# Gated ConvFFN of a two-layer trunk: the order of the seven products and of ScalarE's and VectorE's work in the up-projections

## The chip, the cores and the metric

The kernel runs on one core of one Trainium2 chip. The metric is the device time of one execution in microseconds, the median of several runs. TensorE is called PE, VectorE DVE, ScalarE ACT, GpSimd POOL, and SyncE, whose queue issues nearly all transfers, SP.

## The reference

A trunk of two layers works on 1024 tokens of width 1024, in float32. Layer 0 mixes tokens by a gated linear recurrence, layer 1 by attention over a window. Each layer ends with the part that the change is about, a gated ConvFFN of inner width 2816, followed by a layer norm:

```python
def conv_ffn(h, w_in, conv_w, conv_b, w_out):
    u = h @ w_in
    C = u.shape[-1]
    u = lax.conv_general_dilated(u, conv_w[:, None, :], window_strides=(1,),
                                 padding=[(CONV_WIDTH - 1, 0)],
                                 dimension_numbers=('NWC', 'WIO', 'NWC'),
                                 feature_group_count=C) + conv_b
    a, b = jnp.split(u, 2, axis=-1)
    return (jax.nn.silu(a) * b) @ w_out
```

So `u` (1024 tokens x 5632 channels) is made by a matrix product, each channel is convolved causally with three taps, the first half of the channels goes through SiLU and gates the second half, and a second matrix product goes back to width 1024.

## The kernel before

All products of matrices are made of three matmuls (`mm3`, lines 172 to 177): each operand is held as a high part and a low part in a rounded float32 format, and high x high, high x low and low x high are added in PSUM. The high part is a cast by ACT, the low part a subtraction by DVE (`split`, `low_part`: lines 201 and 148).

The up-projection (class `Up`) handles 22 chunks of 128 channels of each half, so a chunk `fc` gives a 2 x 2 block matrix C: C11 and C21 (the `a` half, for the first and the last 512 tokens; row 0 of a pair of rows of the tile `Y`) and C12 and C22 (the `b` half; row 1). The pair is `Y[:, 0:2]` for even chunks and `Y[:, 2:4]` for odd ones. C is not made of eight block products but of seven, in Strassen's manner (Winograd's form): sums and differences of blocks of the tokens are made once, in `TX` and `TZ`; differences of blocks of the weights are made for each chunk (`weight_sums`, DVE lines 412 to 415, each followed by casts and low parts into `HL` or `HT`). A product is four `mm3`, 12 matmuls of 512 columns. The products are numbered 1 to 7.

From chunk 2 on, the products share PSUM banks (`chained`, line 451). A bank A takes product 1, and then 6, 7 and 4 are added to it in place; after each of them the running sum is copied out by ACT, into C11 (line 457), C12 (463 is the copy into C22 and 461 the one into C12), C22 and C21 (466). PE may not add the next product before the copy has been made. A bank B takes product 2, which DVE adds to C11; a bank M takes product 5, which DVE adds to C22, then product 3 is added to M and DVE adds M to C12. The order in a chunk is 2, 6, 5, 7, then product 1 of the next chunk, 4, 3. Chunks 0 and 1 go another way (`run`, `collect`): each product has a bank of its own, ACT copies product 1 into both C11 and C12, and DVE does all the rest of the additions; product 3 of both chunks comes ahead of product 1 of chunk 2.

When C11 and C21 are there (after product 4), and when C12 and C22 are there (after product 3), `convolve` runs: one tap and the bias by ACT (line 499), two taps by DVE (501), and then SiLU by ACT (504) for the first half, or the product with the gate by DVE (506) and a store to `gd` in HBM for the second. The second half's convolution writes into `C[:, 0]`, the row of C11 and C21 of its own chunk, as scratch.

Beside this, each chunk makes a part of the differences of `ffn_w_out` that the down-projection will need (`down_sums`): load into `Y[:, 6]`, four subtractions of 256 columns by DVE (432), store to `bsd`. `Y[:, 7]` and three tiles `raw` take the loads of the weights (line 403).

PE issues in the order of the source; on ACT, DVE and SP a scheduler decides the order when the kernel is built, guided by priorities (`urgent()`). An engine works through its queue strictly in that order, so an instruction that waits holds up all behind it.

Of the kernel before, what the change touches and what calls it, by code (L numbers as in the profile page):

```python
# [16 lines left out]
P = 128  # L17
# [6 lines left out]
FF = 2816  # L24
# [61 lines left out]
def trunk(ctx: ExitStack, tc: tile.TileContext, a: dict, out: bass.AP):  # L86
# [246 lines left out]
    class Up:  # L333
        def __init__(self, l, pool, rx):
            self.l, self.rx = l, rx
            self.wv = a["ffn_w_in"][l].rearrange("(kc p) c -> p kc c", p=P)
            first = pool.tile([P, 2, 2, 4, 512], F32R, name="TX")
            self.pair = first
            self.TX = [first[:, 0], first[:, 1], pool.tile([P, 2, 4, 512], F32R, name="TZ")]
            self.W, self.raw, self.pieces, self.turned = {}, {}, 0, set()  # L340

# [45 lines left out]
        def weight_load(self, fc):  # L387
# [3 lines left out]
            ws = [whole((0 if fc % 2 else 8) + i) for i in range(7)]  # L391
            self.W[fc] = ws
# [11 lines left out]
            split(blocks(0, 0), blocks(0, 1), r1)  # L404
            self.raw[fc] = blocks, r1, r2

        def weight_sums(self, fc):
            blocks, r1, r2 = self.raw.pop(fc)
            b11, b21, b12, b22 = r1[:, 0], r1[:, 1], r2[:, 0], r2[:, 1]
            ws = self.W[fc]  # L410
            split(ws[6][:, :512], ws[6][:, 512:], b22)
# [4 lines left out]
            split(blocks(1, 0), blocks(1, 1), r1)  # L416
            last = lambda: split(blocks(2, 0), blocks(2, 1), r2)
            if fc:
                last()
            else:  # L420
                self.last = last

        def down_sums(self, n):
            (i, q), pairs = divmod(n, 2), FF // 256
            quarter = lambda rows: rows.rearrange("p (b q n) -> p b q n", b=2, q=2)[:, :, q, :]
            own = Y[:, 6, :].rearrange("p (k b n) -> p k b n", k=2, b=2)
            for k in range(2):
                row = (k * pairs + i) * P
                nc.sync.dma_start(own[:, k], quarter(a["ffn_w_out"][self.l][row:row + P, :]))
            (b11, b12), (b21, b22) = [(own[:, k, 0], own[:, k, 1]) for k in range(2)]  # L430
            for x, y, z in ((b11, b12, b11), (b12, b22, b12), (b22, b22, b11), (b21, b21, b22)):
                tt(x, y, z, op=sub)  # L432
            for k in range(2):
                nc.sync.dma_start(quarter(bsd[self.l][:, i, k, :]), own[:, k])
# [16 lines left out]
        def chained(self, p, fc, banks):  # L451
            A, B, M = banks
# [3 lines left out]
            if p == 1:  # L456
                nc.scalar.copy(C11, A)
            elif p == 2:
                tt(C11, C11, B, op=add)
            elif p == 6:  # L460
                nc.scalar.copy(C12, A)
            elif p == 7:
                nc.scalar.copy(C22, A)  # L463
                tt(C22, C22, M, op=add)
            elif p == 4:
                nc.scalar.copy(C21, A)
            elif p == 3:
                tt(C12, C12, M, op=add)
            if p in (4, 3):
                self.convolve(p, fc, C)  # L470

        def collect(self, p, fc, ps):
            C = Y[:, 2 * (fc % 2):2 * (fc % 2) + 2, :]
            C11, C21, C12, C22 = C[:, 0, :512], C[:, 0, 512:], C[:, 1, :512], C[:, 1, 512:]
            if p == 1:
                nc.scalar.copy(C11, ps)
                nc.scalar.copy(C12, ps)
            elif p == 2:
                tt(C11, C11, ps, op=add)
            elif p == 6:  # L480
                tt(C12, C12, ps, op=add)
            elif p == 7:
                tt(C22, C12, ps, op=add)
            elif p == 4:
                tt(C21, C22, ps, op=add)  # L485
            elif p == 5:
                both = C[:, 1, :].rearrange("p (h n) -> p h n", h=2)
                tt(both, both, ps.unsqueeze(1).to_broadcast([P, 2, 512]), op=add)
            elif p == 3:
                tt(C12, C12, ps, op=add)  # L490
            if p in (4, 3):
                self.convolve(p, fc, C)

        def convolve(self, p, fc, C):
# [3 lines left out]
            c = C[:, 0, :] if part else ca  # L498
            nc.scalar.activation(c, u, AF.Identity, bias=cwt[:, l, 3, ci:ci + 1], scale=cwt[:, l, 2, ci:ci + 1])  # L499
            for sh in (1, 2):  # L500
                nc.vector.scalar_tensor_tensor(c[:, sh:], u[:, :S - sh], cwt[:, l, 2 - sh, ci:ci + 1],  # L501
                                               c[:, sh:], op0=ALU.mult, op1=ALU.add)
            if part == 0:
# [5 lines left out]
        def run(self, ready, down):  # L509
# [5 lines left out]
            for (p, fc), ps in zip([(p, fc) for p in (4, 5) for fc in range(2)], ax):  # L515
                self.product(p, fc, ps)
# [8 lines left out]
            for (p, fc), ps in zip([(p, fc) for p in (1, 2) for fc in range(2)], mm):  # L525
                self.collect(p, fc, self.product(p, fc, ps))
            for fc in range(2):
                self.collect(6, fc, self.product(6, fc, mm[fc]))
            for fc in range(2):
                self.collect(7, fc, self.product(7, fc, mm[2 + fc]))  # L530
                self.collect(4, fc, ax[fc])
                self.collect(5, fc, ax[2 + fc])
            self.weight_load(2)
            for fc in range(2):
                self.product(3, fc, mm[fc])
                if fc == 0:
                    with urgent():
                        self.weight_sums(2)
                self.collect(3, fc, mm[fc])
            banks, n = mm[2:] + ax[:2] + mm[:2] + ax[2:], 0  # L540
            held, made = {}, 0
            todo = [(1, 2)]
            for fc in range(2, NF):
                todo += [(p, fc) for p in (2, 6, 5, 7)] + [(1, fc + 1)] * (fc < NF - 1) + [(4, fc), (3, fc)]
            for p, fc in todo:
                if p == 1 and fc > 2:
                    self.weights(fc)
                if p in (1, 2, 5):
                    held.setdefault(fc, []).append(banks[n % 8])
                    n += 1  # L550
                self.chained(p, fc, (held[fc] + [None, None])[:3])
                if p == 7 or p == 2 and fc in (8, 15):
                    self.down_sums(made)
                    made += 1
                if fc == NF - 1 and p in (2, 5, 4):
# [897 lines left out]
```

## Time and profile before

| | |
|---|---|
| median of 3 runs | 2175.99 us (2174.64 to 2178.3) |
| the profiled execution | 2177.97 us, its span 2175.8 us |
| PE busy | 2133.9 us, 98% |
| DVE busy | 1604.3 us, 74% |
| ACT busy | 934.0 us, 43% |
| granted clock, mean | 0.993 |
| products of the up-projection of layer 0 | 565 to 1003 us of the span |

How to read the rows that follow: a row of the waits says which engine waited, at which line, for which engine and line, how long in total, how often, and the longest. A row of the timeline gives the start in us, the duration, the engine, the line, the operation, what it writes and reads, and in brackets the idle time before it with what ended it. A row of the groups gives the count, the busy time, the mean in ns, and the idle time before. In a row of busy time by stretch stand, after the length, the busy us of each engine with its count of instructions that touch the stretch, then the clock that TensorE was granted, the share of the DMA engines and their rate. A busy PE is not PE at its peak: matmuls overlap, and their rate is read from their starts.

### The profile page before, as it was taken

How to read it: one execution, taken by the hardware profiler on the slowest of the kernel's cores; microseconds unless marked ns; L12 is line 12 of the kernel's file. 1: busy time of each engine (PE TensorE's matmuls, PEld its weight loads, DVE VectorE, ACT ScalarE, POOL GpSimd, SP SyncE). 2: the span in 40 equal slices, each digit the busy share in tenths (PEclk: the TensorE clock that was granted, in tenths of full speed). 3: DMA queues.
4: the chain of work that ended last, by engine and by line, in shares of the span. 5: the costliest groups of instructions: out<-in, count | busy, mean ns of one | idle time of the engine just before them, and what ended most of it. 6: DMA issues, size and time to landing. Idle time of an engine off the chain costs nothing.

```text
span 2175.8 us, 32521 instructions
## 1 busy us (share of the span) xinstructions
PE 2133.9 (98%) x12907; PEld 1788.7 (82%) x12907; DVE 1604.3 (74%) x2170; ACT 934.0 (43%) x1496; POOL 201.3 (9%) x194
## 2 busy tenths in 40 slices
PE   9999999999989999999999999999799999999998
PEld 8888888878868888888788888888688888888887
DVE  3655545468988888887987546769978888878986
ACT  3333333342445444445433246743534444454430
POOL 1221112120100000000001123312000000000002
PEclk9999999999999999999999999999999999999999
DMA  4111111132334444448854411242344444459662
GB/s 161 39 40 40 40 40 35 40 136 78 111 131 136 145 145 141 145 132 282 294 181 164 118 34 36 62 136 78 116 160 133 132 137 145 146 183 321 229 211 97
DMA packets 263698, 278.98 MB, mean 128 GB/s; under 512 B 31481, under 2 KB 201210, under 8 KB 263546
## 3 DMA queue, kind: packets, MB, share of 16 engines
q1 hardware_dynamic: 263032, 276.77, 38.7%
q8 instruction: 101, 1.65, 0.3%
q14 instruction: 51, 0.42, 0.1%
q10 hardware_dynamic: 450, 0.12, 0.0%
q0 software_dynamic: 64, 0.02, 0.0%
HBM read 213.91 MB, written 62.95 MB: 127 GB/s over the span
## 4 chain that ended last, share of the span: by engine, by line
PE 62%; DVE 7%; DMA 3%; issue 1%; ACT 1%; SPq 0%; DVEq 0%; ACTq 0%
PE psmm L174 11%; PE psmm L176 11%; PE psmm L175 11%; PE psax L174 8%; PE psax L175 8%; PE psax L176 8%; PE psmm L180 1%; DVE T L148 1%; PE psax L1232 1%; DVE Y L501 1%; PE psmm L184 1%; DMA raw<-in_ffn_w_out_dram 1%; DVE HL L148 1%; DMA gd<-Y 1%; DMA R<-bsd 1%
## 5 line engine op out<-in xcount | busy, mean ns | idle before, releaser
L174 PE MATMUL psmm<-T,HL 128*128 128x512 f32 x896 | 356.1, 397 | 2.8 <-ACT Y L463 2.8
L176 PE MATMUL psmm<-T,HL 128*128 128x512 f32 x896 | 349.5, 390 | 0.0
L175 PE MATMUL psmm<-T,HL 128*128 128x512 f32 x896 | 349.2, 390 | 0.1
L501 DVE SCALAR_TENSOR_TENSOR Y<-Y,cwt 128x1023 f32<-128x1023 f32 (+1 forms) x176 | 224.5, 1278 | 104.1 <-ACT Y L499 104.1
L148 DVE TENSOR_TENSOR HL<-raw,HL 128x1024 fp32r<-128x1024 f32 x188 | 229.7, 1223 | 64.3 <-ACT HL L155 42.5
L174 PEld LDWEIGHTS psmm<-T,HL 128*128 128x128 f32 x896 | 168.3, 188 | 37.4 <-ACT Y L463 3.6
L176 PEld LDWEIGHTS psmm<-T,HL 128*128 128x128 f32 x896 | 168.2, 188 | 36.0
L175 PEld LDWEIGHTS psmm<-T,HL 128*128 128x128 f32 x896 | 168.4, 188 | 33.8 <-DVE T L148 0.9
L201 ACT CAST HL<-raw 128x1024 fp32r<-128x1024 f32 (+1 forms) x137 | 142.8, 1044 | 121.4 <-DMA raw<-in_ffn_w_in_dram 23.5
L223 POOL TENSOR_TENSOR rs<-rs,nhalf 128x1 f32<-128x1 f32 x32 | 46.0, 1440 | 1431.0 <-DVE rs L222 1431.0
L174 PE MATMUL psax<-T,HL 128*128 128x512 f32 x352 | 137.8, 391 | 0.0
L175 PE MATMUL psax<-T,HL 128*128 128x512 f32 x352 | 137.1, 389 | 0.0
L176 PE MATMUL psax<-T,HL 128*128 128x512 f32 x352 | 137.1, 389 | 0.0
L174 PE MATMUL psmm<-HL,T 128*128 128x256 f32 (+1 forms) x400 | 125.4, 313 | 0.6 <-ACT HL L155 0.6
L176 PE MATMUL psmm<-HL,T 128*128 128x256 f32 (+1 forms) x400 | 122.3, 306 | 0.8 <-DVE T L148 0.8
L175 PE MATMUL psmm<-HL,T 128*128 128x256 f32 (+1 forms) x400 | 122.0, 305 | 0.9 <-DVE HL L148 0.9
L499 ACT ACTIVATE Y<-Y,cwt 128x1024 f32<-128x1024 f32 x88 | 108.6, 1236 | 12.1 <-DVE Y L485 10.8
L432 DVE TENSOR_TENSOR Y<-Y 128x256 f32<-128x256 f32 x176 | 73.8, 419 | 25.2 <-DMA Y<-in_ffn_w_out_dram 24.0
L174 PEld LDWEIGHTS psmm<-HL,T 128*128 128x128 f32 x400 | 76.6, 191 | 5.0 <-ACT HL L155 1.0
L176 PEld LDWEIGHTS psmm<-HL,T 128*128 128x128 f32 x400 | 76.4, 191 | 4.9 <-DVE T L148 1.6
L175 PEld LDWEIGHTS psmm<-HL,T 128*128 128x128 f32 x400 | 76.6, 192 | 4.5 <-DVE HL L148 1.2
L504 ACT ACTIVATE Y<-Y 128x1024 f32<-128x1024 f32 x44 | 46.7, 1061 | 76.3 <-DVE Y L501 76.3
(336 smaller groups left out, 5028.5 us busy)
## 6 DMA issues: line engine op xcount, KB each, us to landing
raw<-in_ffn_w_in_dram SPq DMA_DIRECT2D x136, 256.0 KB
raw<-gd SPq DMA_DIRECT2D x118, 256.0 KB
Y<-in_ffn_w_out_dram SPq DMA_DIRECT2D x88, 256.0 KB
bsd<-Y SPq DMA_DIRECT2D x88, 256.0 KB
gd<-Y SPq DMA_DIRECT2D x44, 512.0 KB
raw<-in_hgrn_w_in_dram SPq DMA_DIRECT2D x32, 512.0 KB
raw<-in_ffn_w_out_dram SPq DMA_DIRECT2D x54, 256.0 KB
R<-bsd SPq DMA_DIRECT2D x44, 256.0 KB
```

Source lines behind the costliest of these rows:

```text
L148: make = lambda e: e.tensor_tensor(lo, src, hi.bitcast(F32), op=ALU.subtract)
L174: nc.tensor.matmul(ps, st(0), mv(0), start=start, stop=False, **free)
L175: nc.tensor.matmul(ps, st(0), mv(1), start=False, stop=False, **free)
L176: nc.tensor.matmul(ps, st(1), mv(0), start=False, stop=stop, **free)
L180: nc.tensor.matmul(ps, lhsT, rhs, start=start, stop=stop, **kw)
L184: nc.tensor.transpose(ps, src, ident)
L201: nc.scalar.copy(hi, src)
L223: nc.gpsimd.tensor_tensor(rs, rs, nhalf, op=ALU.pow)
L432: tt(x, y, z, op=sub)
L499: nc.scalar.activation(c, u, AF.Identity, bias=cwt[:, l, 3, ci:ci + 1], scale=cwt[:, l, 2, ci:ci + 1])
L501: nc.vector.scalar_tensor_tensor(c[:, sh:], u[:, :S - sh], cwt[:, l, 2 - sh, ci:ci + 1], c[:, sh:], op0=ALU.mult, op1=ALU.add)
L504: nc.scalar.activation(c, c, AF.Silu)
```

## The change

It has five parts, all in `Up`.

Chunks 0 and 1 accumulate too: products 6 and 7 are added to product 1's bank and product 3 to product 5's, and after each of 1, 6 and 7 ACT copies the running sum (`collect`, with raised priority), so product 1 is copied once and DVE adds less. Their second convolution uses `Y[:, 6]` as scratch. Product 1 of chunk 2 now comes ahead of product 3 of chunks 0 and 1.

From chunk 3 on the order in a chunk is 6, 5, 7, 2, 4, product 1 of the next chunk, 3.

From chunk 3 on (`chained`) the work that a product sets off on ACT and DVE is put into a region in which these engines too keep the order of the source; each product has a region of its own, and how the regions of different products mix on an engine stays the scheduler's. `convolve` and the making of weights (`weight_steps`) are generators now, whose pieces are placed after chosen products. Chunk 2 and product 1 of chunk 3 go through `begun`, without regions.

Loads: the weights of chunk `fc + 3` are loaded after product 3 of chunk `fc`, and `down_load` starts the load for the next `down_sums` ahead of it. The down sums come after product 4, and in four chunks also after product 7.

The weights that product 3 of chunk 2 uses get a place of their own (`ws[6] = whole(7)`).

The core of the diff, without the bodies that only moved:

```diff
+            if fc == 2:
+                ws[6] = whole(7)
...
         def chained(self, p, fc, banks):
-            A, B, M = banks
+            A, B, M = [banks.get(i) for i in (1, 2, 5)]
...
+            if p == 3:
+                tt(C12, C12, M, op=add)
+                self.second = self.convolve(3, fc, C)
+                if fc + 2 < NF:
+                    self.ahead = ahead = self.weight_steps(fc + 2)
+                    next(ahead)
+                if fc + 3 < NF:
+                    self.weight_load(fc + 3)
+                self.down_load()
             elif p == 6:
                 nc.scalar.copy(C12, A)
+                next(self.second)
+                next(ahead, None)
+                next(self.second)
             elif p == 7:
                 nc.scalar.copy(C22, A)
                 tt(C22, C22, M, op=add)
+                next(ahead, None)
+                while lows:
+                    lows.pop(0)()
+                if fc in (6, 9, 12, 15):
+                    self.down_sums()
+                    self.down_load()
+            elif p == 2:
+                tt(C11, C11, B, op=add)
+                next(self.second, None)
             elif p == 4:
                 nc.scalar.copy(C21, A)
-            elif p == 3:
-                tt(C12, C12, M, op=add)
+                self.silu = self.convolve(4, fc, C)
+                next(self.silu)
+                self.down_sums()
...
         def collect(self, p, fc, ps):
-            if p == 1:
-                nc.scalar.copy(C11, ps)
-                nc.scalar.copy(C12, ps)
+            if p in (1, 6, 7):
+                with urgent():
+                    nc.scalar.copy({1: C11, 6: C12, 7: C22}[p], ps)
...
-            c = C[:, 0, :] if part else ca
+            c = (C[:, 0, :] if fc > 1 else Y[:, 6, :]) if part else ca
...
-            todo = [(1, 2)]
-            for fc in range(2, NF):
-                todo += [(p, fc) for p in (2, 6, 5, 7)] + [(1, fc + 1)] * (fc < NF - 1) + [(4, fc), (3, fc)]
+            todo = [(1, 2), (3, 0), (3, 1)]
+            todo += [(p, 2) for p in (2, 6, 5, 7)] + [(1, 3), (4, 2), (3, 2)]
+            for fc in range(3, NF):
+                todo += [(p, fc) for p in (6, 5, 7, 2, 4)] + [(1, fc + 1)] * (fc < NF - 1) + [(3, fc)]
...
+                    with tc.manual_schedule(engines={EN.PE, EN.Activation, EN.DVE}):
+                        self.chained(p, fc, held[fc])
```

What it moves, at three places of layer 0. The line numbers of the changed kernel are its own: 539 is the copy in `collect`, 524 the one in `begun`, 490, 495, 507 and 515 those of C12, C22, C21 and C11 in `chained`, 558, 561, 565 and 567 the tap by ACT, the taps by DVE, SiLU and the gate.

The first place is ACT's queue at the start of the up-projection, before: from chunk 0's SiLU to the copy of C11 of chunk 2 (psmm_5470 is that chunk's bank A).

```order
L504 ACTIVATE Y_76<-Y_76 128x1024
L201 CAST HT_4828<-raw1_93 128x1024
L499 ACTIVATE Y_76<-Y_76,cwt_81 128x1024
L201 CAST HL_77<-raw0_92 128x1024
L201 CAST HL_77<-Y_76 128x512
L504 ACTIVATE Y_76<-Y_76 128x1024
L499 ACTIVATE Y_76<-Y_76,cwt_81 128x1024 x2
L201 CAST HL_77<-Y_76 128x1024
L201 CAST HL_77<-raw0_92 128x1024
L457 COPY Y_76<-psmm_5470 128x512
```

The same place now, up to the copies of C11 and C12 of chunk 2 (the two L524):

```order
L539 COPY Y_76<-psmm_5468 128x512
L539 COPY Y_76<-psmm_5469 128x512
L558 ACTIVATE Y_76<-Y_76,cwt_81 128x1024 x2
L201 CAST HT_4828<-raw1_93 128x512
L524 COPY Y_76<-psmm_5470 128x512
L565 ACT_TABLE_LOAD
L565 ACTIVATE Y_76<-Y_76 128x1024 x2
L558 ACTIVATE Y_76<-Y_76,cwt_81 128x1024
L201 CAST HL_77<-Y_76 128x512
L201 CAST HL_77<-raw0_92 128x1024
L524 COPY Y_76<-psmm_5470 128x512
```

The copy of C11 stood behind the SiLU of both first chunks and their second convolutions' taps; it stands ahead of both now, and the copy of C12 behind one of those taps.

The second place is DVE's queue there, before: the second convolutions of chunks 0 and 1.

```order
L490 TENSOR_TENSOR Y_76<-Y_76,psmm_5468 128x512
L490 TENSOR_TENSOR Y_76<-Y_76,psmm_5469 128x512
L148 TENSOR_TENSOR HL_77<-Y_76,HL_77 128x512
L432 TENSOR_TENSOR Y_76<-Y_76 128x256
L414 TENSOR_TENSOR Y_76<-Y_76,raw2_94 128x512
L501 SCALAR_TENSOR_TENSOR Y_76<-Y_76,cwt_81 128x1023 x2
L501 SCALAR_TENSOR_TENSOR Y_76<-Y_76,cwt_81 128x1022 x2
L506 TENSOR_TENSOR Y_76<-Y_76 128x1024 x2
```

And now, from the taps of the first convolutions of chunks 0 and 1 (L561, twice two) to the gate of chunk 0:

```order
L561 SCALAR_TENSOR_TENSOR Y_76<-Y_76,cwt_81 128x1023 x2
L561 SCALAR_TENSOR_TENSOR Y_76<-Y_76,cwt_81 128x1022 x2
L548 TENSOR_TENSOR Y_76<-Y_76,psax_5340 128x512
L148 TENSOR_TENSOR HT_4828<-raw1_93,HT_4828 128x512
L548 TENSOR_TENSOR Y_76<-Y_76,psax_5341 128x512
L561 SCALAR_TENSOR_TENSOR Y_76<-Y_76,cwt_81 128x1023
L526 TENSOR_TENSOR Y_76<-Y_76,psmm_5471 128x512
L561 SCALAR_TENSOR_TENSOR Y_76<-Y_76,cwt_81 128x1022
L148 TENSOR_TENSOR HL_77<-Y_76,HL_77 128x512
L567 TENSOR_TENSOR Y_76<-Y_76 128x1024
```

The two second convolutions ran as one block, with both gates behind it; now that of chunk 0 is done first, with the addition of product 2 of chunk 2 (L526) between its taps.

The third place is ACT's queue in a chunk in the middle, before, from one chunk's copy of C11 to the copy of C22:

```order
L457 COPY Y_76<-psax_5340 128x512
L466 COPY Y_76<-psax_5341 128x512
L499 ACTIVATE Y_76<-Y_76,cwt_81 128x1024
L201 CAST HL_77<-Y_76 128x512
L504 ACTIVATE Y_76<-Y_76 128x1024
L499 ACTIVATE Y_76<-Y_76,cwt_81 128x1024
L201 CAST HL_77<-Y_76 128x1024
L201 CAST HL_77<-raw2_94 128x1024
L461 COPY Y_76<-psax_5340 128x512
L201 CAST HL_77<-raw0_92 128x1024
L463 COPY Y_76<-psax_5340 128x512
```

And now, from the tap of the first convolution to the copy of C21 one chunk on:

```order
L558 ACTIVATE Y_76<-Y_76,cwt_81 128x1024
L515 COPY Y_76<-psax_5340 128x512
L565 ACTIVATE Y_76<-Y_76 128x1024
L201 CAST HL_77<-Y_76 128x512
L490 COPY Y_76<-psax_5340 128x512
L558 ACTIVATE Y_76<-Y_76,cwt_81 128x1024
L201 CAST HL_77<-raw2_94 128x1024
L495 COPY Y_76<-psax_5340 128x512
L201 CAST HL_77<-Y_76 128x1024
L201 CAST HL_77<-raw0_92 128x1024
L507 COPY Y_76<-psax_5340 128x512
```

The second convolution's tap (the second L558) now comes after the next chunk's copy of C12 instead of ahead of it, and at most one cast stands between that tap and the copy of C22.

More of the change, by code (lines that the diff above doesn't have):

```diff
@@ L340, in __init__ @@
             self.W, self.raw, self.pieces, self.turned = {}, {}, 0, set()
+            self.lows, self.ahead, self.sums = [], None, list(range(FF // 128))
         def row_loads(self):
@@ L403, in weight_load, with weight_steps @@
                 nc.sync.dma_start(dst.rearrange("p (k c) -> p k c", k=4), self.wv[:, 4 * r:4 * r + 4, c0:c0 + P])
-            split(blocks(0, 0), blocks(0, 1), r1)
             self.raw[fc] = blocks, r1, r2
         def weight_sums(self, fc):
+            steps = self.weight_steps(fc)
+            next(steps)
+            if fc:
+                for _ in steps:
+                    pass
+                while self.lows:
+                    self.lows.pop(0)()
+            else:
+                self.last = lambda: next(steps, None)
+                next(steps)
+                self.lows.pop(0)()
+        def weight_steps(self, fc):
             blocks, r1, r2 = self.raw.pop(fc)
@@ L486, in collect @@
             elif p == 5:
-                both = C[:, 1, :].rearrange("p (h n) -> p h n", h=2)
-                tt(both, both, ps.unsqueeze(1).to_broadcast([P, 2, 512]), op=add)
+                with urgent():
+                    tt(C22, C22, ps, op=add)
             elif p == 3:
@@ L540, in run @@
-            banks, n = mm[2:] + ax[:2] + mm[:2] + ax[2:], 0
-            held, made = {}, 0
-            todo = [(1, 2)]
-            for fc in range(2, NF):
-                todo += [(p, fc) for p in (2, 6, 5, 7)] + [(1, fc + 1)] * (fc < NF - 1) + [(4, fc), (3, fc)]
-            for p, fc in todo:
[L546 to L549, printed above, removed]
-                    n += 1
[L551 to L555, printed above, removed]
+                self.collect(p, fc, self.product(p, fc, ps, group=p == 2))
@@ new lines, in run @@
+            for p in (6, 7):
+                for fc in range(2):
+                    self.collect(p, fc, self.product(p, fc, mm[fc], first=False, group=False))
+                    if p == 7:
+                        self.collect(4, fc, ax[fc])
+                        self.collect(5, fc, ax[2 + fc])
+            self.weights(2)
+            banks, n = mm[2:] + ax[:2] + mm[:2] + ax[2:], 0
+            held = {}
+            todo = [(1, 2), (3, 0), (3, 1)]
+            todo += [(p, 2) for p in (2, 6, 5, 7)] + [(1, 3), (4, 2), (3, 2)]
@@ L556, in run @@
                     down.ahead.append(down.operands(0, len(down.ahead)))
+            for _ in self.second:
+                pass
     class Down:
```

104 lines of the change are left out of this document (65 added, 39 removed).

## The prediction

> **What bounds the kernel now.** I read the page's totals first, then what TensorE (PE) waited for.
>
> ```profile
> span 2175.8 us, 32521 instructions
> ...
> PE 2133.9 (98%) x12907; PEld 1788.7 (82%) x12907; DVE 1604.3 (74%) x2170; ACT 934.0 (43%) x1496; POOL 201.3 (9%) x194
> ```
>
> PE is busy for 98% of the span, and the change leaves it all its matmuls (it only reorders products), so the change can only be worth idle time of PE, or time in which PE ran slowly. The waits of PE, longest first:
>
> ```profile
> PE psmm L174 <- ACT Y L457: 21.4, 2, 10.8
> PE psmm L174 <- ACT Y L463: 2.8, 2, 1.4
> ...
> PE psax L174 <- DVE Y L639: 2.2, 2, 1.6
> PE psmm L175 <- DVE TX L148: 1.1, 2, 0.6
> ```
>
> Two waits of 10.8 us, one in each layer, are half of all idle time; the releaser is the copy of C11 by ScalarE (ACT) in `chained`. PE in order of time there:
>
> ```profile
> 612.26 0.39 PE L176 MATMUL psmm<-T,HL 128*128 128x512 f32 x1
> 623.42 0.80 PE L174 MATMUL psmm<-TX,HT 128*128 128x512 f32 x1 [10.77 <-ACT Y L457]
> 624.01 0.63 PE L175 MATMUL psmm<-TX,HT 128*128 128x512 f32 x1
> 624.44 0.63 PE L176 MATMUL psmm<-TX,HT 128*128 128x512 f32 x1
> ...
> 627.42 0.63 PE L174 MATMUL psmm<-TX,HT 128*128 128x512 f32 x1
> 627.85 0.46 PE L175 MATMUL psmm<-TX,HT 128*128 128x512 f32 x1
> ```
>
> Product 2 of chunk 2 ends at 612.3, product 6 of chunk 2 wants the same bank as product 1 (A), and may not add to it before C11 has been copied out. After the wait, matmuls start 0.43 us apart. What is normal, and what the stall costs, is in the busy time by stretch (in the first two rows PE alone; in the last PE, weight loads, VectorE (DVE), ACT, POOL, then the clock):
>
> ```profile
> 612.26:627.86 15.60, 4.83 (x13) 0.68 0.48 165
> 1566.63:1583.42 16.79, 6.12 (x16) 0.60 0.54 180
> ```
> ```profile
> 640.00:980.00 340.00, 340.00 (x1502) 281.53 (x1501) 280.75 (x358) 164.56 (x199) 0.00 (x0) 1.00 0.43 139
> ```
>
> From 640 to 980 us, 17.9 chunks, PE is never idle: 340/1502 = 0.2264 us a matmul, 2.72 us a product of 12, 19.0 us a chunk of 84. There DVE is busy 83% and ACT 48%. So the steady part has nothing to give, only something to lose; the gain lies at the start of each up-projection.
>
> Why the copy was late:
>
> ```profile
> 615.10 2.36 ACT L499 ACTIVATE Y<-Y,cwt 128x1024 f32<-128x1024 f32 x2
> ...
> 622.78 0.59 ACT L457 COPY Y<-psmm 128x512 f32<-128x512 f32 x1 [3.44 <-DVE Y L506]
> ```
> ```profile
> 616.69 4.86 DVE L501 SCALAR_TENSOR_TENSOR Y<-Y,cwt 128x1023 f32<-128x1023 f32 x4
> 621.47 2.35 DVE L506 TENSOR_TENSOR Y<-Y 128x1024 f32<-128x1024 f32 x2
> ```
>
> The second convolution of chunk 0 uses C[:, 0] as scratch, the rows of Y into which C11 of chunk 2 goes. The copy therefore waits for the product by the gate (L506), that for four taps (L501), and those for product 3, which stood ahead of product 1 of chunk 2.
>
> **The change part by part.** *The stall at the start, one per layer.* In the new order product 1 of chunk 2 comes before product 3 of chunks 0 and 1, and the scratch for these is Y[:, 6]. C11 then depends only on the first convolution of chunk 0. Work goes by these durations (count, busy, mean in ns):
>
> ```profile
> L501 DVE SCALAR_TENSOR_TENSOR Y<-Y,cwt 128x1023 f32<-128x1023 f32 x42 | 53.7, 1281 | 49.8 <-ACT Y L499 49.8
> ...
> L148 DVE TENSOR_TENSOR HL<-raw,HL 128x1024 fp32r<-128x1024 f32 x42 | 51.0, 1217 | 2.8 <-ACT HL L201 2.8
> L432 DVE TENSOR_TENSOR Y<-Y 128x256 f32<-128x256 f32 x83 | 34.8, 419 | 12.9 <-DMA Y<-in_ffn_w_out_dram 12.4
> L506 DVE TENSOR_TENSOR Y<-Y 128x1024 f32<-128x1024 f32 x21 | 25.5, 1217 | 0.0
> ...
> L468 DVE TENSOR_TENSOR Y<-Y,psmm 128x512 f32<-128x512 f32 x10 | 6.8, 680 | 0.0
> ```
> ```profile
> L499 ACT ACTIVATE Y<-Y,cwt 128x1024 f32<-128x1024 f32 x42 | 51.8, 1236 | 5.7 <-DVE Y L485 5.1
> L201 ACT CAST HL<-raw 128x1024 fp32r<-128x1024 f32 x43 | 45.1, 1049 | 10.1 <-PE psmm L175 4.3 <-PE psax L175 4.1 <-DVE raw L415 1.7
> L504 ACT ACTIVATE Y<-Y 128x1024 f32<-128x1024 f32 x21 | 22.3, 1061 | 38.1 <-DVE Y L501 38.1
> ...
> L457 ACT COPY Y<-psmm 128x512 f32<-128x512 f32 x10 | 5.9, 587 | 21.1 <-PE psmm L176 17.7 <-DVE Y L506 3.4
> ...
> L504 ACT ACT_TABLE_LOAD x1 | 1.3, 1283 | 1.0 <-DVE Y L501 1.0
> ```
>
> Neighbours overlap by about 0.1 us (four taps take 4.86, not 5.1), so I take 1.2 for a tap, 1.14 for a low part or the gate product, 0.6 for an addition or subtraction of 512, 0.34 for a down sum; on ACT 1.14, 0.95, 0.96 and 0.49.
>
> I walk the opening with the products 2.72 apart, anchored at two starts that come before anything that the change moves:
>
> ```profile
> 590.82 0.50 PE L175 MATMUL psmm<-TX,HT 128*128 128x512 f32 x1 [0.49 <-DVE TX L148]
> ```
> ```profile
> 595.28 1.06 ACT L201 CAST HL<-raw 128x1024 fp32r<-128x1024 f32 x1 [6.08 <-DMA raw<-in_ffn_w_in_dram]
> ```
>
> The first is product 6 of chunk 0; the 0.5 us wait stays, since the cast ahead of it is released by PE as before. So product 7 of chunks 0 and 1 starts at 596.2 and 598.9, product 1 of chunk 2 at 601.6, product 3 at 604.3 and 607.1, products 2, 6, 5, 7 of chunk 2 at 609.8, 612.5, 615.2 and 618.0. Now each new need:
> - Product 7 of chunk 1 adds to bank A after product 6: C12 must be copied first. On ACT that copy stands behind the cast that waits for raw2 (595.28) and one more: 595.28 + 2 x 0.95 + 0.6 = 597.8, 1.1 us early.
> - Product 3 of chunk 0 adds to the bank of product 5, which DVE must have read into C22. The cast for product 7's old weights, the copy of C22 and two additions follow product 7's end: about 602.6 for 604.3.
> - Product 6 of chunk 2 needs C11. The copy stands behind a cast into the weights that product 3 of chunk 0 reads to 607.1: done at 608.2, 4 us early. This is the wait that cost 10.8.
> - Product 7 of chunk 2 needs C12 of chunk 2, whose place is read by the second convolution of chunk 0: table load 609.4, two SiLUs 611.4, ACT's tap 612.6, two taps on DVE with one addition between to 615.7, copy 616.4, for 618.0. Slack 1.5.
> - Product 7 of chunk 3, at 634.3, needs a copy that stands behind SiLU and ACT's tap of chunk 2. DVE runs without a pause from 612.6: I get 631.2 for the taps before that SiLU, and 633.9 for the copy. Slack 0.4, the thinnest.
>
> All five hold. For the last and the first I allow 0.75 us a layer (between 0 and twice that), as they have least room.
>
> The stall of layer 1, for the sum:
>
> ```profile
> 1577.70 0.79 PE L174 MATMUL psmm<-TX,HT 128*128 128x512 f32 x1 [10.67 <-ACT Y L457]
> ```
>
> What goes: from 612.26 to 627.85 there are 11 steps (12 starts) in 15.6 us, worth 11 x 0.2264 = 2.5, so 13.1 is lost; in layer 1, 14 steps in 16.8, worth 3.2, 13.6 lost. Together **26.7**, of which 21.4 is waiting and 5.3 the half clock after it and the latency of the first matmul. The row of the clock reads 0.68 and 0.60 over those stretches. The Trainium skill, "TensorE: Matmul & The Clock Gate", section "What's actually happening", has the clock halved after an idle window of about 3.4 us, and back after 3.4 us of work; by that figure the slow part would cost 1.6 us a layer, and the total would be 2 us less; the trace shows half speed for 4.4 and 5.7 us (623.42 to 627.85, 1577.70 to 1583.42), and I use the trace.
>
> *The end of each up-projection.* Product 2 now stands between 7 and 4 of the last chunk.
>
> ```profile
> 995.37 0.39 PE L176 MATMUL psmm<-TZ,HL 128*128 128x512 f32 x1
> 997.15 0.50 PE L174 MATMUL psmm<-T,HL 128*128 128x512 f32 x1 [1.39 <-ACT Y L463]
> 997.49 0.40 PE L175 MATMUL psmm<-T,HL 128*128 128x512 f32 x1
> ```
>
> The copy of C22 gets 2.72 us more, 1.39 were missing: **2.8** for both layers. A cast for the down-projection still stands ahead of that copy.
>
> *The down-projection* is not edited, but the new order of DVE puts its evacuation of product 2 two additions and two low parts earlier (3.5 us). The wait on L639 above, 1.65 and 0.6, should go: **2.2**, or 0 if DVE is held by a load there.
>
> *The steady chunk.* DVE's work stays: 4 taps, 4 of 1.14, 8 of 0.6, 4 of 0.34, 15.5 us of 19.0; ACT's stays too. What changes is what stands ahead of PE's releases. Each copy that PE needs (C12 after product 6, C22 after 7, C11 after 1) has one product of 2.72 us between, as before in all but the last chunk. Counted from a chunk's start, with the order shown in the section on the change: the copy of C12 at 2.9 to 3.5, the convolution's tap to 4.6, the cast of the next weights when DVE has made the four differences (5 to 6), the copy of C22 at 8.3 to 8.9 for product 4 at 10.9, C21 and the tap to 15.4, C11 at 16.4 to 17.0 for product 6 at 19.0. Slack about 2. The loads of a chunk's weights are emitted three chunks ahead, and have most of a chunk to land before the first cast wants them; a late one holds up ACT only beyond that. Where down sums stand between the four differences, DVE may wait for their load:
>
> ```profile
> 630.33 1.28 SPq L434 DMA_DIRECT2D bsd<-Y  x2
> 633.19 1.22 SPq L429 DMA_DIRECT2D Y<-in_ffn_w_out_dram  x2
> ```
> ```profile
> 636.34 0.42 DVE L432 TENSOR_TENSOR Y<-Y 128x256 f32<-128x256 f32 x1 [1.00 <-DMA Y<-in_ffn_w_out_dram]
> ```
>
> From the store to the next sum are 6.0 us. Two groups of sums in a chunk then leave the fourth difference at about 8.1, the cast at 9.1 and C22 at 9.7: slack 1.2. I cost it at nothing; uncovered it would be about 1 us in some four chunks a layer, which the range holds.
>
> The sum: 2177.97 (the profiled execution; its span 2175.8 and 2.2 around it) - 26.7 - 2.8 - 2.2 + 1.5 = 2147.8. The median of the runs shown is 2.0 below this execution, so **2146** for the median.
>
> **The rivals.**
> - *Forecast, 0.66*: 2142 to 2151, by the waits just bounded.
> - *A smaller wait takes the stall's place, 0.20.* For: five needs in a row with 0.4 to 1.8 us to spare, all on ACT's queue, which also holds casts that wait for DMA; the load above made ACT wait 6.1 us. Against: the loads for chunks 4 and 5 are issued sooner. If a load is that late, 6.1 - 1.1 = 5 us a layer and up to 2.5 of slow clock: 2 x 7.5 = 15, 2161; half of that is likelier, 2154.
> - *Every chunk pays, 0.09, slower.* On ACT a weight cast stands ahead of the copy of C22 in each chunk, and waits for DVE's differences, which are now interleaved with taps and sums. If that copy is late by 1 us past its slack, 38 chunks cost 38 us: 2146 + 38 = 2184. It decides from 0.8 us a chunk. Against it: DVE has 3.5 us to spare in a chunk. The Trainium skill, same page, section "A second HAM failure mode: psum-queue depth-cycling", would add a falling clock to such short pauses; after the 1.39 us wait above the matmuls went on at 0.34 and 0.23, so the trace does not show it, and 2184 is without it.
> - *It does not do what it says, 0.05*: C11 is held by something else as long (the ynd store or load of that row): within 0.2% of 2176.
>
> **How the numbers follow.** Faster by over 0.2% (4.4 us, about what a measurement of this kernel can tell from no change): 0.66 + 0.20 = 0.86; within: 0.05; slower: 0.09. The range goes from 2142 (no new wait, and the lowest run 1.4 below the median) to 2161, the moved wait at its worst; the last two cases stay outside, and a little of each of the others.
>
> **What would show it.** Right: no wait of PE over 2 us in either up-projection, the clock 1.00 in both, no wait for the copy of C22 at their ends, and from 640 to 980 still about 1502 matmuls. Wrong: a wait of PE on L524 or L539 of several us with a dip of the clock (second case); idle PE on L495 or L490 spread over the chunks (third); L524 for C11 of chunk 2 late and released by DVE (fourth).

## The result and the profile after

The changed kernel takes 2152.15 us in the median (2148.37 to 2156.06), the kernel before on the same chip 2176.91 (2174.64 to 2178.30). The ratio is 0.9887, with a 95% interval of 0.9867 to 0.9908. The profiled execution took 2151.38 us. The forecast was 2146, its range 2142 to 2161; the forecast's own case, without a new wait, was 2142 to 2151.

The totals of the changed kernel's page, and the longest waits of PE in it:

```profile
span 2149.3 us, 32472 instructions
...
PE 2131.1 (99%) x12907; PEld 1786.3 (83%) x12907; DVE 1611.5 (75%) x2162; ACT 939.9 (44%) x1500; POOL 201.1 (9%) x194
```
```profile
PE psmm L913 <- DVE cwt L914: 2.3, 1, 2.3
PE psax L174 <- ACT Y L495: 2.0, 4, 0.9
...
PE psax L174 <- DVE Y L709: 0.4, 1, 0.4
PE psax L174 <- ACT Y L490: 0.2, 1, 0.2
```

The two waits of 10.8 us for C11 are gone, and so are the two of 1.4 for the copy of C22 at the ends. The longest wait now (L913) lies in the layer's setup and was there before. New are four short waits on L495, the copy of C22, and one of 0.2 us on L490, the copy of C12. ACT and PE in order of time at the place of the old stall:

```profile
609.68 0.59 ACT L524 COPY Y<-psmm 128x512 f32<-128x512 f32 x1 [0.51 <-DVE Y L561]
...
617.95 0.59 ACT L524 COPY Y<-psmm 128x512 f32<-128x512 f32 x1 [1.76 <-DVE Y L561]
```
```profile
614.01 0.39 PE L174 MATMUL psmm<-TX,HT 128*128 128x512 f32 x1
...
619.45 0.39 PE L174 MATMUL psmm<-TZ,HT 128*128 128x512 f32 x1
```

C11 of chunk 2 is out at 610.27 and product 6 starts without a wait at 614.01; C12 is out at 618.54 and product 7 starts at 619.45. The busy time by stretch of the changed kernel (PE, weight loads, DVE, ACT, POOL, clock):

```profile
590.00:640.00 50.00, 49.41 (x217) 40.29 (x216) 44.24 (x52) 27.47 (x33) 0.00 (x0) 1.00 0.35 110
...
640.00:980.00 340.00, 339.28 (x1495) 280.12 (x1494) 289.05 (x368) 166.14 (x197) 0.00 (x0) 1.00 0.48 154
1594.00:1934.00 340.00, 338.69 (x1491) 279.37 (x1491) 287.72 (x361) 164.39 (x195) 0.00 (x0) 1.00 0.47 154
```

The opening runs at full clock. The steady stretch does 1495 and 1491 matmuls where it did 1502 and 1501: a little was given back there.

Where the time went, by starts of matmuls in the traces (stretches in us; the last column is a second profiled execution of the changed kernel, from a later measurement):

| stretch | before | after | after, again |
|---|---|---|---|
| up-projection of layer 0, from product 6 of chunk 0 to the first matmul of the down-projection | 412.78 | 399.87 | 401.95 |
| the same in layer 1 | 413.47 | 400.20 | 401.25 |
| down-projection and norm of layer 0, to the attention | 268.49 | 266.79 | 268.37 |
| from the down-projection of layer 1 to the end | 218.04 | 217.82 | 218.88 |

The up-projections gave 26.2 us in the one and 23.1 in the other, the down-projections 1.9 and -0.7. Outside the change 1.7 us were lost in the first profile, in the setup of layer 0: the clock was at half there for some 6.9 us around 395 us, where the second profile had about 3.4 us of it at the same place and the kernel before about 3.4 us around 469 us.

### The profile page after: what moved, and what is told of

Read it like the earlier page. It is cut to its first block, busy times and chain, and to the rows that moved or that the text cites. A ratio compares the mean times of both kernels' runs of the same rounds, so it can differ in the third digit from the quotient of the medians.

```text
span 2149.3 us, 32472 instructions
## 1 busy us (share of the span) xinstructions
PE 2131.1 (99%) x12907; PEld 1786.3 (83%) x12907; DVE 1611.5 (75%) x2162; ACT 939.9 (44%) x1500; POOL 201.1 (9%) x194
## 3 DMA queue, kind: packets, MB, share of 16 engines
q8 instruction: 101, 1.65, 0.3%
## 4 chain that ended last, share of the span: by engine, by line
PE 83%; DVE 9%; DMA 5%; issue 1%; ACT 1%; SPq 0%; DVEq 0%; ACTq 0%
PE psmm L174 17%; PE psmm L175 17%; PE psmm L176 17%; PE psax L174 8%; PE psax L176 8%; PE psax L175 8%; PE psax L180 3%; DMA Y<-in_ffn_w_out_dram 2%; DVE HL L148 2%; DMA bsd<-Y 2%; DVE Y L561 1%; PE psmm L184 1%; PE psmm L180 1%; PE psax L184 1%; PE psax L1302 1%
## 5 line engine op out<-in xcount | busy, mean ns | idle before, releaser
L148 DVE TENSOR_TENSOR HL<-raw,HL 128x1024 fp32r<-128x1024 f32 (+1 forms) x190 | 230.9, 1218 | 61.4 <-ACT HL L155 43.1
L561 DVE SCALAR_TENSOR_TENSOR Y<-Y,cwt 128x1022 f32<-128x1022 f32 (+1 forms) x176 | 225.0, 1281 | 33.4 <-ACT Y L558 31.9
L558 ACT ACTIVATE Y<-Y,cwt 128x1024 f32<-128x1024 f32 x88 | 109.4, 1245 | 9.2 <-DVE Y L504 4.3
L174 PEld LDWEIGHTS psax<-T,HL 128*128 128x128 f32 x352 | 66.1, 188 | 17.0 <-ACT Y L495 3.6
```

Source lines behind the costliest of these rows:

```text
L148: make = lambda e: e.tensor_tensor(lo, src, hi.bitcast(F32), op=ALU.subtract)
L174: nc.tensor.matmul(ps, st(0), mv(0), start=start, stop=False, **free)
```

## The experiments

Theory S was mine: the scratch of the second convolution, which lay where C11 of chunk 2 goes, makes the stall. Its rivals put it on the order of the products (O) or on DVE's work in chunks 0 and 1 (A).

**The scratch alone**, in the kernel before:

```diff
-            c = C[:, 0, :] if part else ca
+            c = (C[:, 0, :] if fc > 1 else Y[:, 6, :]) if part else ca
```

> The kernel before with one change: the second convolutions of chunks 0 and 1 use Y[:, 6] as scratch in place of C[:, 0]. Theory S (the scratch holds C11 of chunk 2, and nothing else of the opening matters much): the copy of C11 now stands behind the second SiLU and two casts, done at about 612 us, so the wait of 10.8 us per layer goes; the next one, the copy of C12 behind the second convolution of chunk 0, leaves 1.5 to 3 us a layer. Time 2152 to 2160. Theory O (product 3 of chunks 0 and 1 ahead of product 1 of chunk 2 is what holds the copy; only the 3.4 us that it waited for the gate is the scratch's): 2168 to 2172.

Measured: 2155.84 us against 2179.09, ratio 0.9899 (0.9884 to 0.9914). Its waits of PE, and the copy of C11 of chunk 2 on ACT:

```profile
PE psmm L174 <- ACT Y L461: 3.9, 3, 1.8
PE psax L174 <- DVE Y L639: 2.9, 2, 2.0
PE psmm L174 <- ACT Y L463: 2.8, 2, 1.4
```
```profile
609.74 0.57 ACT L457 COPY Y<-psmm 128x512 f32<-128x512 f32 x1
```

One line takes away the whole wait for C11. Without the false dependence the scheduler itself puts the copy of C11 ahead of the second convolutions. What is left is C12 (L461: 1.75 and 1.30 us in the two openings, 0.87 in chunk 6 of layer 0) and the two waits that this line does not touch. O falls. The new order alone can't be tried: with the old scratch, the second convolution of chunk 0 would write over C11 of chunk 2, which would already be there.

**The accumulation and the steady part, without scratch and order**:

```diff
-            c = (C[:, 0, :] if fc > 1 else Y[:, 6, :]) if part else ca
+            c = C[:, 0, :] if part else ca
...
-            todo = [(1, 2), (3, 0), (3, 1)]
+            todo = [(3, 0), (3, 1), (1, 2)]
```

> The changed kernel with the old opening order (product 3 of chunks 0 and 1 ahead of product 1 of chunk 2) and the old scratch; it keeps the accumulation in chunks 0 and 1 and all of the steady part. Theory S: the copy of C11 waits for the gate of chunk 0 again, which DVE reaches at about 617 since it has less to read; the wait of PE is 5 to 6.5 us a layer instead of 10.8, and some of the slow clock is back: 2163 to 2170. Theory A (the accumulation in chunks 0 and 1, which takes work off DVE, is what removes the stall): 2150 to 2156, no wait over 2 us.

Measured: 2172.72 us, ratio 0.9972 (0.9963 to 0.9982). The waits of PE, the copy of C11, and PE's restart:

```profile
PE psmm L174 <- ACT Y L524: 10.3, 2, 5.2
PE psax L174 <- DVE Y L709: 2.9, 2, 1.6
PE psax L174 <- DVE Y L546: 2.8, 2, 1.5
```
```profile
620.62 0.59 ACT L524 COPY Y<-psmm 128x512 f32<-128x512 f32 x1 [3.54 <-DVE Y L567]
```
```profile
615.71 0.39 PE L176 MATMUL psmm<-T,HL 128*128 128x512 f32 x1
621.26 0.79 PE L174 MATMUL psmm<-TX,HT 128*128 128x512 f32 x1 [5.16 <-ACT Y L524]
621.85 0.63 PE L175 MATMUL psmm<-TX,HT 128*128 128x512 f32 x1
...
626.40 0.40 PE L174 MATMUL psax<-T,HL 128*128 128x512 f32 x1
```

The copy waits for the gate (L567) again. DVE, with less to read, reaches it sooner, so the stall is 5.2 us instead of 10.8; with half clock until 626.2 it costs 10.7 us for 13 steps worth 2.9, so 7.7 us a layer. A falls: the accumulation shortens the stall and does not remove it. The time is 3 us above what I had expected from S. S does not speak of the waits on L709 and L546, nor of those on L495, the copy of C22, in the steady part, which come to 4.1 us.

**Order and scratch, without the accumulation**, in the kernel before (the lines that call the products in the new order left out here):

```diff
+            if fc == 2:
+                ws[6] = whole(7)
...
-            c = C[:, 0, :] if part else ca
+            c = (C[:, 0, :] if fc > 1 else Y[:, 6, :]) if part else ca
...
-            todo = [(1, 2)]
+            todo = [(1, 2), (3, 0), (3, 1)]
```

> The kernel before with the new opening order (product 1 of chunk 2 ahead of product 3 of chunks 0 and 1) and Y[:, 6] as scratch, and a place of its own for the weights of product 3 of chunk 2; chunks 0 and 1 do not accumulate, and the steady part is the old one. Theory S: the stall goes as in the changed kernel, and the waits at the end of the up-projections (2.8) and in the down-projection (2.2) stay: 2150 to 2156. Theory A: DVE, with more to read in chunks 0 and 1, is too late for the copy of C12 of chunk 2 and a wait of 3 us or more a layer is left: 2158 or more.

Measured: 2156.11 us, ratio 0.9897 (0.9882 to 0.9911): the order adds nothing to the scratch that these intervals could show, and the accumulation is not needed. The trace shows a little: PE waits for no copy in the two openings now, where the scratch alone left 1.75 and 1.30 us. But three waits for C12 stand in chunks 4 and 6 (1.25, 1.31 and 1.58 us), so the sum is about the same.

**The end of the up-projection**: product 7 directly ahead of product 4 in the last chunk.

```diff
-                todo += [(p, fc) for p in (6, 5, 7, 2, 4)] + ...
+                todo += [(p, fc) for p in ((6, 5, 7, 2, 4) if fc < NF - 1 else (6, 5, 2, 7, 4))] + ...
```

> The changed kernel, but in the last chunk product 7 stands directly ahead of product 4, as before (order 6, 5, 2, 7, 4, 3). Theory of the prediction (product 2 between 7 and 4 is what removed the wait at the end of each up-projection): a wait of PE for the copy of C22 of about 1.4 us comes back at the end of each up-projection, 3 to 4 us in all with the latency. Rival (the wait went because no cast stands late ahead of that copy any more): no wait there over 0.4 us and the time of the changed kernel.

Measured: 2157.43 us, ratio 0.9899 (0.9883 to 0.9916), not told apart from the changed kernel by time. The trace decides: at 985.6 and 1927.3 us stands a step of 1.78 us each, a wait of 1.4 for the copy of C22, as before the change. In its waits of PE they are the two longest of this row:

```profile
PE psmm L174 <- ACT Y L495: 3.7, 3, 1.4
```

The prediction's step holds, and the rival falls: product 2 between 7 and 4 is worth these 2.8 us of waiting.

**Without the regions**: ACT and DVE left to the scheduler from chunk 3 on.

```diff
-                    with tc.manual_schedule(engines={EN.PE, EN.Activation, EN.DVE}):
+                    with tc.manual_schedule(engines={EN.PE}):
```

> The changed kernel, but from chunk 3 on only PE is held to the order of the source; ACT and DVE are left to the scheduler, which now puts the second convolution's tap and a cast ahead of the copy of C12. Theory N (the steady part has slack, so the order on ACT and DVE there is worth nothing): the copy is done 1.3 us before product 7 needs it, and the time is within 3 us of the changed kernel, 2149 to 2155. Rival C (the steady part is held at its rate only by this order): waits of PE on the copies of C12 or C22 of 0.3 to 1 us in most of 37 chunks, 2162 to 2190.

Measured: 2170.88 us, ratio 0.9961 (0.9950 to 0.9973). I had believed N; it falls. C's time comes true, and its picture in part: 17 waits on the copy of C12, of 0.5 to 2.5 us, where it had 0.3 to 1 us in most of 37 chunks. PE's waits, and one of them on DVE, ACT and PE:

```profile
PE psmm L174 <- ACT Y L490: 10.1, 9, 2.5
PE psax L174 <- ACT Y L490: 8.8, 8, 2.3
```
```profile
748.71 0.42 DVE L455 TENSOR_TENSOR Y<-Y 128x256 f32<-128x256 f32 x1 [3.69 <-DMA Y<-in_ffn_w_out_dram]
749.05 1.28 DVE L561 SCALAR_TENSOR_TENSOR Y<-Y,cwt 128x1022 f32<-128x1022 f32 x1
750.24 1.34 DVE L455 TENSOR_TENSOR Y<-Y 128x256 f32<-128x256 f32 x3
751.50 0.68 DVE L481 TENSOR_TENSOR Y<-Y,psax 128x512 f32<-128x512 f32 x1
```
```profile
752.22 1.24 ACT L558 ACTIVATE Y<-Y,cwt 128x1024 f32<-128x1024 f32 x1 [0.23 <-DVE Y L481]
753.54 1.04 ACT L201 CAST HT<-raw 128x1024 fp32r<-128x1024 f32 x1
754.49 0.58 ACT L490 COPY Y<-psmm 128x512 f32<-128x512 f32 x1
```
```profile
755.13 0.50 PE L174 MATMUL psmm<-TZ,HL 128*128 128x512 f32 x1 [2.45 <-ACT Y L490]
```

Read backwards: PE waits for the copy of C12, which stands on ACT behind the second convolution's tap of the chunk before, which waits for C12's addition (L481) on DVE, which stands behind a down sum that waits 3.69 us for its load. The load can't start before the store of the group before it has left the same place, `Y[:, 6]`; SyncE's queue waits for such stores up to 4.7 us.

The small waits of the changed kernel have the same root. DVE, ACT and PE of the changed kernel in chunk 19 of layer 0:

```profile
939.15 0.43 DVE L455 TENSOR_TENSOR Y<-Y 128x256 f32<-128x256 f32 x1 [2.95 <-DMA Y<-in_ffn_w_out_dram]
939.50 0.68 DVE L481 TENSOR_TENSOR Y<-Y,psmm 128x512 f32<-128x512 f32 x1
...
945.50 0.69 DVE L431 TENSOR_TENSOR raw<-raw,raw 128x512 f32<-128x512 f32 x1
```
```profile
946.22 1.05 ACT L201 CAST HL<-raw 128x1024 fp32r<-128x1024 f32 x1 [4.76 <-DVE raw L431]
947.18 0.57 ACT L495 COPY Y<-psax 128x512 f32<-128x512 f32 x1
```
```profile
947.81 0.50 PE L174 MATMUL psax<-T,HL 128*128 128x512 f32 x1 [0.53 <-ACT Y L495]
```

So theory L: what the steady part loses, with regions or without, is the wait of DVE for the load of the down sums. Three runs test it.

**No down sums, and no regions**: the edit of the run without regions, and the four subtractions left out, loads and stores kept.

```diff
             for x, y, z in ((b11, b12, b11), (b12, b22, b12), (b22, b22, b11), (b21, b21, b22)):
-                tt(x, y, z, op=sub)
+                pass
```

> The kernel without regions for ACT and DVE, and without the four subtractions of each group of down sums. Without regions PE waited 18.9 us on the copy of C12. Theory L (DVE waits for the load of the down sums ahead of taps and of C12's addition, 3.7 us at the longest, and the copy of C12 stands behind that on ACT): the waits go to under 3 us, and the time to within 3 us of the changed kernel's. Rival Q (the copy of C12 behind the second convolution's tap and a cast is late by itself): waits on the copy of C12 stay at 10 us or more, time 2160 to 2170.

Measured: 2150.04 us, ratio 0.9864 (0.9849 to 0.9878). PE's waits on L490 fall from 18.9 us to 2.9:

```profile
PE psax L174 <- ACT Y L490: 2.9, 3, 1.5
```

Q falls as the main cause; the 2.9 us are all of its size. That DVE has 1.4 us a chunk less to do is part of this run too.

**No down sums, with the regions**: the same edit in the changed kernel.

> The changed kernel without the four subtractions of each group of down sums (the loads and stores stay), so DVE has 1.4 us a chunk less and never waits for these loads. Theories L and W: no wait of PE on the copies of C12 or C22 is left in either up-projection; 2 to 4 us under the changed kernel. If waits of that size stay, neither the load nor DVE's work is their cause.

Measured: 2149.58 us, ratio 0.9860 (0.9846 to 0.9875); none of the waits on L495 is among its waits of PE. One of 0.5 us on the copy of C12 (L490, product 7 of chunk 3) stays, against the expectation, and two new ones on the copy of C11 come (0.2 and 1.2 us):

```profile
PE psax L174 <- ACT Y L515: 1.4, 2, 1.2
...
PE psax L174 <- ACT Y L490: 0.5, 1, 0.5
```

By the ratios it is 6 to 8 us below the changed kernel, where 2 to 4 were expected; the two were not run on one chip. With the sums left out, the kernels with and without regions take the same on one chip (2149.58 and 2150.04 us), so without the sums the regions give nothing that shows.

**The down sums behind the taps**: the sums kept, but emitted in the region of product 1, behind the first convolution's taps. In the region of product 4 they were the only work of DVE, and floated.

```diff
             elif p == 4:
                 nc.scalar.copy(C21, A)
                 self.silu = self.convolve(4, fc, C)
                 next(self.silu)
-                self.down_sums()
...
             elif p == 1:
                 nc.scalar.copy(C11, A)
                 next(self.silu)
                 next(self.silu, None)
+                self.down_sums()
```

> The changed kernel with the down sums of a chunk emitted behind the taps of the first convolution (after product 1 of the next chunk) in place of after product 4, so that on DVE they can't be placed ahead of those taps. Theory L (the small waits that are left, 2.0 us on the copy of C22, come from DVE waiting for the load of the down sums ahead of C12's addition): DVE waits for that load 19.5 us in layer 0 now, then under 6, the waits on the copy of C22 go, and the time is 2 to 4 us under the changed kernel's. Rival W (it is DVE's work ahead of the weight differences, not the load, that makes the copy late): the sums stand nearer ahead of the differences now, and the waits on the copy of C22 grow to 4 us or more.

Measured: 2148.03 us (2147.64 to 2148.83), ratio 0.9855 (0.9840 to 0.9870). DVE's wait for that load in the up-projection of layer 0, and the busy time by stretch:

```profile
DVE Y L455 <- DMA Y<-in_ffn_w_out_dram: 6.3, 5, 1.9
```
```profile
640.00:980.00 340.00, 339.78 (x1498) 280.74 (x1497) 291.09 (x371) 166.58 (x197) 0.00 (x0) 1.00 0.48 155
1594.00:1934.00 340.00, 340.00 (x1502) 281.40 (x1501) 290.40 (x366) 167.60 (x197) 0.00 (x0) 1.00 0.49 160
```

DVE waits 6.3 us for the load where the changed kernel's waits show 19.5 (19 times), and PE does 1498 and 1502 matmuls in the steady stretch. No wait of PE over 0.15 us on the copy of C22 is left. W falls: the work is the same, only its place and that of the waiting have changed.

**The changed kernel and this one again, side by side on one chip**:

> The changed kernel as it is, on one chip with the next two for the comparison. Ratio to the kernel before as first measured, 0.987 to 0.991.

> The kernel with the down sums behind the taps, again, beside the changed kernel on one chip. Theory L: PE had no wait of note left in the up-projections, so it is 2 to 4 us (0.1 to 0.2%) below the changed kernel here too. Rival (the first measurement was another chip's doing): the same as the changed kernel within 1 us.

Measured: the changed kernel 2156.10 us (2152.75 to 2157.69), ratio 0.9898 (0.9883 to 0.9912); with the sums behind the taps 2148.80 (2148.38 to 2149.40), ratio 0.9867 (0.9851 to 0.9884). Every run of the second lies below every run of the first; 7.3 us between the medians, more than expected. The waits of PE in the changed kernel's second profile show where:

```profile
PE psax L174 <- DVE Y L709: 3.0, 2, 1.5
PE psax L174 <- ACT Y L495: 2.4, 4, 1.2
...
PE psmm L174 <- ACT Y L495: 1.2, 2, 0.8
```

The same kernel waits 3.6 us on L495 here, and 2.0 in its first profile, and 3.0 on L709 where it had 0.4; the other kernel's second profile has 0.4 on L495 and 0.8 on L709. The changed kernel's runs spread by 5 to 8 us, those with the sums behind the taps by 1.2 at most. A load that lands just before or just after DVE wants it would make such a spread; that it comes from this load alone was not tried.

**Two lines alone**: the kernel before with the new scratch and, in the last chunk only, the order 6, 5, 7, 2, 4, 3.

```diff
-            c = C[:, 0, :] if part else ca
+            c = (C[:, 0, :] if fc > 1 else Y[:, 6, :]) if part else ca
...
-                todo += [(p, fc) for p in (2, 6, 5, 7)] + ...
+                todo += [(p, fc) for p in ((2, 6, 5, 7) if fc < NF - 1 else (6, 5, 7, 2))] + ...
```

The other lines of this edit only keep the banks by the number of their product.

> The kernel before with two lines changed: the scratch of the second convolutions of chunks 0 and 1, and the order of the last chunk (6, 5, 7, 2, 4, 3). Theory S (these two carry the gain, and the accumulation in chunks 0 and 1, the order of the other chunks and the regions give nothing more): 2152 to 2156 where the kernel before takes 2179, within 2 us of the changed kernel. Rival (the rest of the change is worth more than 4 us): 2157 or more.

Measured: 2153.78 us, ratio 0.9888 (0.9874 to 0.9903), 2.3 us below the changed kernel on the same chip and not told apart from it. Its longest waits of PE in the up-projections:

```profile
PE psmm L174 <- ACT Y L461: 4.3, 3, 1.5
```

S holds: these two lines carry the gain. The rest of the change takes away these waits on C12 (1.55 and 1.33 us in the openings, 1.38 in chunk 6) and brings those on C22 and L709.

**More work on DVE**, to measure the room in a chunk:

```diff
                 tt(C12, C12, M, op=add)
+                for _ in range(4):
+                    tt(C12, C12, C12, op=ALU.max)
```

> The changed kernel with four more operations of 512 columns on DVE in each chunk from 3 on, right behind C12's addition (2.4 us a chunk; they leave the values as they are). DVE was busy 289 of 340 us, 16.2 a chunk of 19.0. Theory of the prediction (DVE has some 3 us to spare in a chunk, the copies of C12 and C22 about 2): DVE is busy 98%, and waits of 0.3 to 0.8 us a chunk come up, 2165 to 2185. Rival (the room is much smaller): 1.5 us or more a chunk, 2205 or more. If the time stays within 5 us of the changed kernel's, the room was larger than reckoned.

Measured: 2174.38 us, ratio 0.9983 (0.9974 to 0.9993). Busy time by stretch:

```profile
640.00:980.00 340.00, 335.15 (x1471) 275.21 (x1469) 319.92 (x428) 159.23 (x193) 0.00 (x0) 1.00 0.45 144
```

DVE is busy 94%, not 98%, since it still waits for loads; 340 us hold 1471 matmuls, 31 fewer than before, 7.0 us or 0.4 a chunk. The size is as reckoned, and the time, 18.3 us above the changed kernel on the same chip, lies in the expected range; but the waits are mostly on the copy of C11, 9.0 us in 11, and in the profiles 7.5 us of the difference lie in the down-projections, where PE waits 2.9 and 3.5 us for the addition that is L709 in the changed kernel. The scheduler also moved casts behind the copy of C22 in this kernel, so it is no clean measure of that copy's slack.

## Why the prediction was right, and where it was off

*The number.* The median, 2152.15 us, lies in the range, but 1 us above the forecast's own band of 2142 to 2151, and the second measurement, 2156.10, 5 us above it. The range reached so far for the rival of a moved wait, which is not what happened, so that the range held is in part luck; the cause that did come, a late load of the down sums, was named as one that the range would hold. The gain is 24.8 and 22.0 us where 30 were forecast: the mechanism was right, and a term put at nothing was not nothing.

*The stall, -26.7.* Right in place and size: the scratch makes it, and it goes entirely. With the sums behind the taps, where PE has hardly a wait left, the up-projections are 29.7 and 29.3 us shorter than before, in its two profiles; the sum has 26.7 + 2.8 = 29.5 for the stall and the ends. Of my walk, the copies of C11 and C12 of chunk 2 came out 0.4 and 0.5 us later than reckoned, once 1.65 us are taken off for the later start of the whole up-projection (591.59 against 589.94). I had put the removal on the order and the scratch together; the order was not needed.

*The ends, -2.8.* Right, and shown from both sides, by the waits.

*The down-projection, -2.2, "or 0 if DVE is held by a load there".* It is both: PE waits 0.4 us on L709 in one profile and 3.0 in the other, more than the 2.2 of before. In layer 1 of the second, DVE waits 0.35 and 0.51 us for loads from `gd` shortly ahead of it; that this is the whole cause is not shown.

*New waits, +1.5, for two thin links.* The first, product 7 of chunk 1, never waited. The one called the thinnest, product 7 of chunk 3, waits 0.2 us in one profile and 0.3 in the other, in layer 0 alone. So this term was too large.

*The steady chunk, at nothing, slack "about 2" and 1.2 in chunks with two groups of sums.* This is the step that failed in size. From the end of the copy of C22 to product 4, the first profile shows 1.93 us at the most, but a median of 1.21 in layer 0 and 0.87 in layer 1 over 19 chunks, and nothing left in several. I had named the cause, a late load of the down sums, and allowed it 1 us in some four chunks a layer, in the range but not in the sum; it costs 2.0 to 3.6 us of waiting on L495 over both layers, and against the kernel with the sums behind the taps the up-projections are 3.4 and 6.5 us longer. The place was wrong: in the first profile the waits are in chunks 7 and 19 of layer 0 and 8 and 19 of layer 1, not in those with two groups (6, 9, 12, 15). The sums float on DVE, and one that waits stands ahead of C12's addition of the chunk before. Without the sums this slack is 1.93 us in 17 of 19 chunks of each layer, so it is the sums that narrow it. Two groups in a chunk do matter, but one chunk later: with the sums behind the taps the slack is at most 0.64 us in chunks 7, 10, 13 and 16, each behind one with two groups, and 1.2 or more in all others.

So the up-projections gave 26.2 and 23.1 us where the sum had 28.0, and the down-projections 1.9 and -0.7 where it had 2.2. Against the sum of 2147.8 the two profiled executions took 2151.4 and 2155.3 us; of these 3.6 and 7.5 us, 2.1 and 7.9 lie in these terms, and in the first 1.7 in the setup, outside the change.

*The rivals.* That a smaller wait takes the stall's place did not come true in the opening. That every chunk pays did not come true either; some chunks pay a little, on the copy that was named. In the changed kernel this hangs on the regions: without them 17 waits on C12 bring some 15 us of the 22 to 25 back, by another mechanism than the one I had described. The kernel with two lines alone has no regions and pays 1.38 us in its steady part, so the regions mostly make good what the rest of the change brings in.

## What to carry to other kernels

A scratch buffer that lies in the place of a later result is a wait in disguise: look at what the late copy overwrites before reordering anything, since one line may be the whole gain. An off-path job that loads, computes and stores in one buffer should be emitted behind work of its own engine that is on the path, or its wait for the load will sometimes stand ahead of that work. A term that one's own range admits ("a few chunks, 1 us each") belongs in the sum at half its size.

## What the runs showed of the hardware

How short an idle time brings PE's clock down. In the run without regions, one wait of 2.27 us (until 817.14) was followed by matmuls at full rate until 818.4 and then at half clock for 3.4 us; another of 2.45 us (until 755.13) was not. Busy time by stretch in that run:

```profile
752.20:758.00 5.80, 3.35 (x16) 2.43 (x15) 5.76 (x7) 3.83 (x4) 0.00 (x0) 1.00 0.44 141
814.40:818.40 4.00, 1.73 (x8) 1.09 (x7) 3.97 (x5) 3.58 (x4) 0.00 (x0) 1.00 0.59 186
818.40:822.10 3.70, 3.70 (x11) 2.87 (x10) 3.70 (x5) 0.57 (x2) 0.00 (x0) 0.54 0.30 88
```

The wait of 2.3 us in the setup of layer 0 (L913) did the same in the first profile of the changed kernel: 7.5 us at a mean clock of 0.54, so half clock for some 6.9 us of them. The same wait of 2.3 us stands in all 14 profiles, and half clock followed it, for 3.4 or 6.9 us, in 12; in the kernel before and with the scratch alone (L843 there) it did not.

```profile
394.00:401.50 7.50, 7.50 (x53) 6.38 (x56) 1.62 (x7) 0.00 (x0) 0.00 (x0) 0.54 0.46 133
```

In the up- and down-projections no profile shows the clock lowered after a wait of 2.0 us or less. That is no floor: in the setup of layer 0 of the kernel before, half clock followed two waits of 0.63 and 0.90 us that stand close together (until 464.81 and 466.21). In this row stand the busy time of PE alone, the clock and the DMA:

```profile
467.50:471.00 3.50, 3.50 (x42) 0.51 0.39 140
```

The Trainium skill, "TensorE: Matmul & The Clock Gate", section "What's actually happening", puts the idle window at about 3.4 us, and the work that brings the clock back at one such window or more. Here 2.3 us of idle time were enough, some of the time; the slow parts of 3.4 and 6.9 us are about one and two of its windows. The 17 waits of the run without regions brought one such dip, and the clock of its steady stretch was 0.99.
